# w_out as seven block products per pair of chunks in a decoder layer on one Trainium2 core

## The chip, the core and the metric

The kernel runs on one core of a Trainium2 chip. The metric is the device time of one execution in microseconds, taken as the median of several runs. Names of engines: PE is TensorE, DVE is VectorE, ACT is ScalarE, POOL is GpSimd and SP is SyncE, which only issues transfers here.

## The reference

The reference is one decoder layer on 256 tokens of width 2048 in float32: a half-step SwiGLU feed-forward stage, a mixer of two attention branches, a second feed-forward stage, each followed by a layer norm. Cut to the part that changes:

```python
h = _layer_norm(ALPHA * h + 0.5 * _swiglu(h, ffn1_w_gate, ffn1_w_up, ffn1_w_down), ln1_g, ln1_b)
...
y = sigmoid(gate_mla) * (o_mla @ w_br_mla) + sigmoid(gate_diff) * (o_diff @ w_br_diff)
mix = y @ w_out                       # (256, 2048) @ (2048, 2048)
h = _layer_norm(ALPHA * h + mix, ln2_g, ln2_b)
h = _layer_norm(ALPHA * h + 0.5 * _swiglu(h, ffn2_w_gate, ffn2_w_up, ffn2_w_down), ln3_g, ln3_b)
```

## The kernel before

**Products.** The 256 tokens are two halves, b = 0 and 1. A matrix product runs over chunks of 512 output columns and over units of two k tiles (256 rows of the weight matrix). Every float32 operand is split into a high part, rounded by ACT (L149), and a low rest, subtracted by DVE (L150). `triple` (L202 to L204) then issues three matmuls of 128x128 by 128x512 for each pair of tiles, so a unit has 12 matmuls for both halves.

**Units.** `project` makes a chunk out of units. Each unit has a load of 512 KB on SP's queue (L227), a preparation (the split into a pair of tiles taken from a ring) and its products. The ring holds 6 pairs in the mixer and w_out, and more (`widen`) where the products for b = 1 run behind those for b = 0 by `lag` units, so that the layer norm of b = 0 lies beside the products of b = 1. `look` says how many units are loaded and prepared ahead. `later(n, f)` puts a step n units further down the program. The framework may still order ready instructions of an engine among each other.

**Seven block products.** In the gate and up projections of the feed-forward stages two chunks are made together. `Seven` and `Hybrid` treat k tiles 0 to 7 as a 2x2 block product (two token halves, two groups of four k tiles, two chunks) done in seven products instead of eight, and k tiles 8 to 15 as plain units. `Seven` makes the sums of activation blocks in five steps (tiles `fa`, `fb`, `xs`). `Hybrid.group` loads the weight blocks 11, 12, 21 and 22 into `sraw` (two tiles each), adds blocks on DVE (L316: 12 and 22 and 21 onto others, eight additions of 128x1024 a group), splits them, and copies four partial results out of the PSUM banks X and Z with ACT (`snap`, L293 and L294), which `done` later adds or subtracts. The two halves s = 0, 1 of a block product have 6 matmuls each.

**Turning.** The results of some projections stand with tokens in rows and are needed with tokens in columns. `turn` does this by DMA: DVE transposes blocks of 32x32 (L405), four transfers of POOL's queue write them to DRAM (L407), one reads them back (L419), and a number of units later ACT or DVE uses them (L427 or L149). `rows_to_quad` does it on PE instead, four transposes to a quad of four k tiles (L370).

**Mixer and w_out.** The mixer projects q, k, v and the gates and does the attention heads between the units. `branch(f)`, for f = 0 to 3, multiplies the branch results by the gates on DVE (L892, L895, L896) and gives 512 columns of y, which is quad f of the input of w_out: quads 0 to 2 are turned by DMA, quad 3 by PE. Then all pending steps are flushed, and w_out is four chunks of eight plain units. `LayerNorm` loads the residual z (L445, scaled by ACT at L446) and the gain and bias `gb` (L450); `evac` adds a bank to z and takes its statistics (L464, L468); after the last chunk of a half `apply` norms it and transposes it for the second feed-forward stage.

Of the kernel before, what the change touches and what calls it, by code (L numbers as in the profile page):

```python
# [11 lines left out]
F32 = mybir.dt.float32  # L12
# [6 lines left out]
P = 128  # L19
# [11 lines left out]
G = 2  # L31
# [28 lines left out]
def layer_kernel(ctx: ExitStack, tc: tile.TileContext, a: dict, out: bass.AP):  # L60
# [212 lines left out]
    class Hybrid:  # L273


        def __init__(self, x, seven, k_tiles):
            self.x, self.seven, self.k_tiles = x, seven, k_tiles
            self.raws = {n: [act_tile([P, 1024], F32, "sraw") for _ in range(2)] for n in ("11", "12", "21", "22")}
            self.snaps = [[act_tile([P, 2, 512], F32, "snap") for _ in range(2)] for _ in range(2)]
            self.turn = 0  # L280

        def group(self, w0, w1, done):
            banks = {}
            snap = [t[:, i, :] for t in self.snaps[self.turn % 2] for i in range(2)]
            self.turn += 1
            n1, n2, n3, q5 = snap
# [9 lines left out]
                     4: lambda: done(0, 1, banks["W"], n3, ALU.subtract)}  # L296
            stops = {1, 5, 6, 7, 2, 4}
# [7 lines left out]
            def seventh(p, s):  # L305
                load_block, src, add, b = plan[p]
                st = {}

                def load():
                    w, j0 = blocks[load_block]  # L310
                    nc.sync.dma_start(R[load_block][s], w[j0 + s])

                def prep():
                    t = R[src][s]
                    if add is not None:
                        V.tensor_tensor(out=t, in0=t, in1=R[add[1]][s], op=ALU.add)  # L316
                    pair = next_pair()
                    split(*pair, t)
                    st["pair"] = [v.rearrange("p (g n) -> p g n", g=G) for v in pair]

                def now():
                    o, first = bank(b)
                    wh, wl = st["pair"]
                    xh, xl = self.seven.at_[p]
                    for g in range(G):
                        k = 2 * s + g
                        triple(o, xh[:, k, :], xl[:, k, :], wh[:, g, :], wl[:, g, :], first and g == 0,
                               s == 1 and g == 1 and p in stops, b in "XZ")
                    if s == 1 and p in after:
                        after[p]()  # L330
                unit(load if load_block else None, prep, now)

            def plain(n, j, last=False):
# [12 lines left out]

                def now():
                    wh, wl = st["pair"]
                    for b in range(2):
                        o, first = bank(names[b])  # L350
                        for g in range(G):
                            k = 2 * j + g
                            triple(o, self.x.at(0, k, b), self.x.at(1, k, b), wh[:, g, :], wl[:, g, :],
                                   first and g == 0, last and g == 1, n == 1)
                    if last:
                        done(1, 0, banks["Z"], n2, ALU.add)
                        done(1, 1, banks["X"], q5, ALU.add)
                unit(load, prep, now)
# [54 lines left out]
    def turn(row, use, wait):  # L413
# [9 lines left out]
    def turn_to_quad(row, b, x, q, wait):  # L423
        turn(row, lambda t: x.put(q, b, t), wait)

    def turn_to_cols(row, dst, b, wait):
        turn(row, lambda t: S.copy(dst[:, :, b * P:(b + 1) * P].rearrange("p k (i c) -> p k i c", i=4), t), wait)  # L427

    class LayerNorm:
# [28 lines left out]
        def evac(self, c, b, bank):  # L458
# [10 lines left out]
            if c == 3:  # L469
                self.apply(b)  # L470

# [232 lines left out]
    def mixer(x):  # L704
# [8 lines left out]
        def c_norm(b, i):  # L713
# [9 lines left out]
            later(2, lambda: turn_to_quad(c, b, cn, i, 6))  # L723
# [23 lines left out]
        def cols_proj(w, xx, kt, name, k0=0):  # L747
# [22 lines left out]
        def qr_done(b, bank):  # L770
# [3 lines left out]
            later(1, lambda: turn_to_cols(t, qrT, b, 5))  # L774
        project(a["wuq"][2], cn, 4, 512, qr_done)
        kT = [cols_proj(a["wuk"][c], cn, 4, "kT", 4) for c in range(2)]
# [111 lines left out]
        def branch(f):  # L888
# [5 lines left out]
            def done1(b, bank):  # L894
                V.tensor_tensor(out=g1[:, b, :], in0=bank, in1=g1[:, b, :], op=ALU.mult)  # L895
                V.tensor_tensor(out=g0[:, b, :], in0=g0[:, b, :], in1=g1[:, b, :], op=ALU.add)  # L896
                if f < 3:
                    later(1, lambda: turn_to_quad(g0[:, b, :], b, yq, f, 4))
# [10 lines left out]
        for f in range(4):  # L909
            branch(f)  # L910
# [70 lines left out]
def _layout(i):  # L981
# [29 lines left out]
    r["w_out"] = _chunks(np.concatenate([_turned_rows(w["w_out"][:1536]), w["w_out"][1536:]]), 512)  # L1011
# [34 lines left out]
```

## Time and profile before

| What | Value |
|---|---|
| Median of three runs | 2028.31 us (2028.13, 2028.31, 2032.78) |
| Profiled execution | 2032.79 us, its span 2031.0 us |
| Instructions | 25081, of them 8976 matmuls |
| Busy share of the span | PE 99%, DVE 75%, ACT 57%, POOL 11% |
| Mean granted TensorE clock | 0.995 |
| DMA | 446.84 MB, mean 220 GB/s |

A row of groups gives line, engine, operation, tiles and count, then the busy time, the mean of one in ns and the idle time before it. A row of a window gives start and end, the length, the busy times with counts of PE, PEld (weight loads), DVE, ACT and POOL, the granted clock, the busy share of the DMA engines and GB/s. A row of waits gives who waited for whom, the sum in us, the count and the longest. A row of DMA issues ends with the KB of one and the median time from issue to landing in us. A busy PE is not a PE at its peak: the modelled duration of a matmul overlaps the next one.

### The profile page before, as it was taken

Reading aid. Unit: us, or ns where it says so; the run is one execution under the profiler, and the core shown is the slowest. Engines: PE = TensorE matmul, PEld = TensorE weight load, DVE = VectorE, ACT = ScalarE, POOL = GpSimd, SP = SyncE. Lnnn points to the kernel's source line nnn. Section 1 sums busy time; section 2 is a strip of 40 time slices with the busy share of each in tenths; the row PEclk is TensorE's granted clock in tenths of the full one; section 3 lists DMA queues with packets and bytes.
Section 4 is the critical chain, followed back from the end, with each engine's and each line's share of the span. In section 5 each row is a group of like instructions: output and inputs, shape, how many; then the busy total and the mean of one; then the engine's idle time right before and its main releaser. Section 6 shows DMA issues by size and latency. Waiting matters only on the chain.

```text
span 2031.0 us, 25081 instructions
## 1 busy us (share of the span) xinstructions
PE 2005.3 (99%) x8976; PEld 1660.6 (82%) x8976; DVE 1529.2 (75%) x1793; ACT 1151.6 (57%) x1443; POOL 224.1 (11%) x419
## 2 busy tenths in 40 slices
PE   8999999999999999999999999999999999999997
PEld 7788888887888888888888887878888888888886
DVE  6999999997554686665665555699999999964555
ACT  5666666666333565555674445476666666653332
POOL 0111001112000012620001100001100110220000
PEclk9999999999999999999999999999999999999999
DMA  8766766668655757964456667666776667686664
GB/s 285 233 221 222 243 227 200 214 219 300 206 193 192 245 186 242 301 227 156 156 175 213 214 202 267 214 234 220 244 241 226 198 213 239 206 308 190 196 196 136
DMA packets 129501, 446.84 MB, mean 220 GB/s; under 512 B 18704, under 2 KB 18784, under 8 KB 129376
## 3 DMA queue, kind: packets, MB, share of 16 engines
q1 hardware_dynamic: 108000, 387.50, 57.0%
q0 software_dynamic: 20224, 55.65, 8.7%
q10 hardware_dynamic: 1152, 2.10, 0.3%
q8 instruction: 70, 1.15, 0.2%
q14 instruction: 55, 0.45, 0.1%
HBM read 420.00 MB, written 25.17 MB: 219 GB/s over the span
## 4 chain that ended last, share of the span: by engine, by line
PE 93%; DMA 3%; DVE 1%; ACT 1%; issue 1%; POOL 0%; DVEq 0%; ACTq 0%; SPq 0%; POOLq 0%
PE mm L202 30%; PE mm L203 30%; PE mm L204 30%; DMA xraw<-in_xT_dram 1%; DMA gb<-in_ln_g_dram 1%; DMA turned<-turn 1%; DVE wring L150 1%; ACT wring L149 0%; PE tr L370 0%; DMA sraw<-in_gu_dram 0%; DMA z<-res 0%; PE tr L791 0%; PE tr L820 0%; PE tr L789 0%; DVE sraw L316 0%
## 5 line engine op out<-in xcount | busy, mean ns | idle before, releaser
L150 DVE TENSOR_TENSOR wring<-raw,wring 128x1024 fp32r<-128x1024 f32 (+1 forms) x582 | 701.8, 1209 | 410.3 <-ACT wring L149 405.6
L149 ACT CAST wring<-raw 128x1024 fp32r<-128x1024 f32 (+1 forms) x582 | 604.5, 1043 | 541.8 <-PE mm L204 465.7
L202 PE MATMUL mm<-wring,h 128*128 128x512 f32 (+2 forms) x1632 | 634.3, 389 | 0.3 <-ACT wring L149 0.3
L204 PE MATMUL mm<-wring,h 128*128 128x512 f32 (+2 forms) x1632 | 630.1, 386 | 0.0
L203 PE MATMUL mm<-wring,h 128*128 128x512 f32 (+2 forms) x1632 | 629.3, 386 | 0.8 <-DVE wring L150 0.8
L203 PEld LDWEIGHTS mm<-wring,h 128*128 128x128 f32 x1632 | 306.7, 188 | 62.3 <-DVE wring L150 2.0
L204 PEld LDWEIGHTS mm<-wring,h 128*128 128x128 f32 x1632 | 306.6, 188 | 62.2 <-DVE h L150 1.0
L202 PEld LDWEIGHTS mm<-wring,h 128*128 128x128 f32 x1632 | 306.7, 188 | 61.6 <-ACT h L149 1.0
L149 ACT CAST wring<-sraw 128x1024 fp32r<-128x1024 f32 x280 | 290.2, 1052 | 110.7 <-PE mm L204 68.9
L150 DVE TENSOR_TENSOR wring<-sraw,wring 128x1024 fp32r<-128x1024 f32 x280 | 335.1, 1219 | 8.3 <-ACT wring L149 6.0
L202 PE MATMUL mm<-wring,xs 128*128 128x512 f32 x560 | 218.7, 391 | 2.0 <-ACT snap L293 2.0
L203 PE MATMUL mm<-wring,xs 128*128 128x512 f32 x560 | 218.5, 390 | 0.0
L204 PE MATMUL mm<-wring,xs 128*128 128x512 f32 x560 | 218.3, 390 | 0.0
L316 DVE TENSOR_TENSOR sraw<-sraw,sraw 128x1024 f32<-128x1024 f32 x160 | 191.8, 1214 | 0.1
L407 POOL DMA_DIRECT2D hT<-blocks x176 | 95.5, 551 | 744.4 <-DVE blocks L405 740.1
L202 PE MATMUL mm<-wring,x 128*128 128x512 f32 x384 | 150.1, 392 | 4.8 <-ACT x L149 4.8
L203 PE MATMUL mm<-wring,x 128*128 128x512 f32 x384 | 150.1, 392 | 0.6 <-DVE wring L150 0.6
L204 PE MATMUL mm<-wring,x 128*128 128x512 f32 x384 | 149.9, 391 | 0.0
L202 PEld LDWEIGHTS mm<-wring,xs 128*128 128x128 f32 x560 | 105.5, 188 | 24.2 <-ACT snap L293 2.4
L204 PEld LDWEIGHTS mm<-wring,xs 128*128 128x128 f32 x560 | 105.5, 188 | 22.0
L203 PEld LDWEIGHTS mm<-wring,xs 128*128 128x128 f32 x560 | 105.6, 188 | 21.9
L407 POOL DMA_DIRECT2D turn<-blocks x112 | 61.0, 552 | 378.2 <-DVE blocks L405 347.8
(238 smaller groups left out, 1621.5 us busy)
## 6 DMA issues: line engine op xcount, KB each, us to landing
raw<-in_gu_dram SPq DMA_DIRECT2D x192, 512.0 KB, 4.3
raw<-in_dn_dram SPq DMA_DIRECT2D x176, 512.0 KB, 4.2
sraw<-in_gu_dram SPq DMA_DIRECT2D x160, 512.0 KB, 5.2
raw<-in_wgm_dram SPq DMA_DIRECT2D x32, 512.0 KB, 3.3
raw<-in_wgd_dram SPq DMA_DIRECT2D x32, 512.0 KB, 3.6
raw<-in_w_out_dram SPq DMA_DIRECT2D x32, 512.0 KB, 3.5
hT<-blocks POOLq DMA_DIRECT2D x176, 64.0 KB, 2.5
hraw<-hT POOLq DMA_DIRECT2D x44, 256.0 KB, 3.9
```

The source lines that it names most:

```text
L149: S.copy(hi, src)
L150: V.tensor_tensor(out=lo, in0=src, in1=hi.bitcast(F32), op=ALU.subtract)
L202: PE.matmul(o, xh, wh, start=first, stop=False, skip_group_check=again)
L203: PE.matmul(o, xh, wl, start=False, stop=False, skip_group_check=again)
L204: PE.matmul(o, xl, wh, start=False, stop=last, skip_group_check=again)
L316: V.tensor_tensor(out=t, in0=t, in1=R[add[1]][s], op=ALU.add)
L407: nc.gpsimd.dma_start(to.rearrange("(g r) (i f) -> i r g f", g=4, i=4)[i], t[32 * i:32 * (i + 1), :].rearrange("r (g f) -> r g f", g=4))
```

## The change

- w_out becomes two groups of two chunks by `Hybrid.group`, with seven block products for k tiles 0 to 7 and plain units for k tiles 8 to 15. Quads 0 and 1 of y are turned by DMA and kept as raw tiles for `Seven`; quad 2 is now turned by PE like quad 3. The host lays out w_out's rows accordingly.
- There are no snaps in w_out. `LayerNorm.fold` adds or subtracts a partial result from bank X or Z to z on DVE, right after products 1, 6, 7 and 5.
- Half of the block sums are made by adding transfers: after the preparation of product 5 a transfer of POOL's queue adds block 22 from DRAM onto the tile of block 12 (for product 7), after that of product 6 block 21 onto the tile of block 11 (for product 4).
- The layer norm and `Seven` are set up before the last branch, with a ring of 5; nothing is flushed between the branch and w_out. In the last group the plain units of the second chunk come last, the products for b = 1 four units behind those for b = 0.
- In `turn` the transfer back is issued `wait` units on, and the use follows `more` units after it: 4 and 10 (8 for k, 8 for the normed q and kv rows) instead of 4 and 5 (5 and 6); the heads start two units later.

```diff
     class Hybrid:
-        def __init__(self, x, seven, k_tiles):
+        def __init__(self, x, seven, k_tiles, snaps=True, adds=None):
+            self.adds = adds or {}
...
-        def group(self, w0, w1, done):
+        def group(self, w0, w1, done, fold=None, last_group=False):
...
+            if fold is not None:
+                after = {1: lambda: fold(0, 0, banks["X"], -1.0), 6: lambda: fold(1, 0, banks["X"], 1.0),
+                         7: lambda: fold(0, 1, banks["X"], -1.0), 5: lambda: fold(1, 1, banks["Z"], 1.0),
+                         2: lambda: done(0, 0, banks["Y"]), 4: lambda: done(0, 1, banks["W"])}
...
-                    if add is not None:
+                    if add is not None and (src, add[1]) not in self.adds.values():
                         V.tensor_tensor(out=t, in0=t, in1=R[add[1]][s], op=ALU.add)
                     pair = next_pair()
                     split(*pair, t)
...
+                    if p in self.adds:
+                        to, block = self.adds[p]
+                        w, j0 = blocks[block]
+                        nc.gpsimd.dma_start(R[to][s], w[j0 + s], accum_op=ALU.add)
...
+                if last_group and n == 1:
+                    unit(load, prep, lambda: half(0), lambda: half(1))
+                else:
+                    unit(load, prep, now)
...
+            if last_group:
+                for p, js in ((1, (4,)), (5, (5,)), (6, (6,)), (7, (7,)), (2, ()), (4, ()), (3, ())):
+                    for s in range(2):
+                        seventh(p, s)
+                    for j in js:
+                        plain(0, j)
+                look(0, 0)
+                lag[0] = 4
+                for j in range(4, end + 1):
+                    plain(1, j, j == end)
+                return
...
-    def turn(row, use, wait):
+    def turn(row, use, wait, more):
...
-            later(wait, lambda: use(turned(t)))
-        later(wait - 1, back)
+            later(more, lambda: use(turned(t)))
+        later(wait, back)
...
+        def fold(self, c, b, bank, sign):
+            z = self.z[b][c // 2][:, (c % 2) * 512:(c % 2) * 512 + 512]
+            V.scalar_tensor_tensor(out=z, in0=bank, scalar=sign * self.scale, in1=z, op0=ALU.mult, op1=ALU.add)
...
-            later(2, lambda: turn_to_quad(c, b, cn, i, 6))
+            later(2, lambda: turn_to_quad(c, b, cn, i, 4, 8))
...
-                later(1, lambda: turn_to_cols(t, dst, b, 5))
+                later(1, lambda: turn_to_cols(t, dst, b, 4, more))
...
-                later(10 + 3 * h + 2 * i, f)
+                later(12 + 3 * h + 2 * i, f)
...
-                if f < 3:
-                    later(1, lambda: turn_to_quad(g0[:, b, :], b, yq, f, 4))
+                if f < 2:
+                    later(1, lambda: turn(g0[:, b, :], lambda t: S.copy(
+                        yq.raw(f, b).rearrange("p (k i c) -> p k i c", k=4, i=4), t), 4, 6))
...
         for f in range(4):
+            if f == 3:
+                before_last(yq)
             branch(f)
...
-    yq = mixer(h1)
-    catch_up(0)
-    flush()
     h2 = Acts(KD, "h2", (0, 1))
-    ln = LayerNorm(1.0, res[0], a["ln2_g"], a["ln2_b"], keep(1), h2, (a["ln2_gc"], a["ln2_bc"]))
-    for c in range(4):
-        project(a["w_out"][c], yq, KD, 512, lambda b, bank, c=c: ln.evac(c, b, bank),
-                hook=at_unit(0, widen) if c == 3 else None)
+    out_stage = {}
+
+    def before_out(y):
+        narrow_to(5)
+        out_stage["ln"] = LayerNorm(1.0, res[0], a["ln2_g"], a["ln2_b"], keep(1), h2, (a["ln2_gc"], a["ln2_bc"]), (0, 16))
+        seven = out_stage["seven"] = Seven(y)
+        for i, f in enumerate(seven.steps):
+            later(2 + i, f)
+
+    yq = mixer(h1, before_out)
+    ln = out_stage["ln"]
+    narrow_to(6)
+    look(3, 4)
+    hy = Hybrid(yq, out_stage["seven"], KD, False, {5: ("12", "22"), 6: ("11", "21")})
+    for p in range(2):
+        hy.group(a["w_out"][2 * p], a["w_out"][2 * p + 1], lambda n, b, bank, p=p: ln.evac(2 * p + n, b, bank),
+                 lambda n, b, bank, sign, p=p: ln.fold(2 * p + n, b, bank, sign), p == 1)
+    widen()
```

More of the change, by code (lines that the diff above doesn't have):

```diff
@@ L345, in prep, with half @@
                     st["pair"] = [v.rearrange("p (g n) -> p g n", g=G) for v in pair]
-                def now():
[L348 to L358, printed above, removed]
-            end = self.k_tiles // G - 1
+                def half(b):
+                    wh, wl = st["pair"]
+                    o, first = bank(names[b])
+                    for g in range(G):
+                        k = 2 * j + g
+                        triple(o, self.x.at(0, k, b), self.x.at(1, k, b), wh[:, g, :], wl[:, g, :],
+                               first and g == 0, last and g == 1, n == 1)
+                    if last and fold is not None:
+                        done(1, b, o)
+                    elif last:
+                        done(1, b, o, (n2, q5)[b], ALU.add)
+                def now():
+                    half(0)
+                    half(1)
+                if last_group and n == 1:
+                    unit(load, prep, lambda: half(0), lambda: half(1))
+                else:
+                    unit(load, prep, now)
+            end = self.k_tiles // G - 1
+            if last_group:
[9 more added lines that the diff above has]
+                return
             for p, n, j in ((1, 0, 4), (5, 0, 5), (6, 0, 6), (7, 0, 7), (2, 1, 4), (4, 1, 5), (3, 1, 6)):
@@ L702, in p_cols, with mixer @@
         return pt
-    def mixer(x):
+    def mixer(x, before_last):
         c_row = [act_tile([P, 1024], F32, "c_row") for _ in range(2)]
```

24 lines of the change are left out of this document (13 added, 11 removed).

## The prediction

> **What bounds the kernel now.** I read the page first: its table of busy times and the chain that ended last. Then PE's waits, then the windows and timelines of PE and DVE around the stage that changes, then the table of DMA issues.
>
> ```profile
> PE 2005.3 (99%) x8976; PEld 1660.6 (82%) x8976; DVE 1529.2 (75%) x1793; ACT 1151.6 (57%) x1443; POOL 224.1 (11%) x419
> ...
> PE mm L202 30%; PE mm L203 30%; PE mm L204 30%; DMA xraw<-in_xT_dram 1%; DMA gb<-in_ln_g_dram 1%; DMA turned<-turn 1%; DVE wring L150 1%; ACT wring L149 0%; PE tr L370 0%; DMA sraw<-in_gu_dram 0%; DMA z<-res 0%; PE tr L791 0%; PE tr L820 0%
> ```
> Nine tenths of the chain are the three matmul lines L202 to L204. So a microsecond is worth something only where PE issues fewer matmuls or stands still less. PE's idle time against others is short:
>
> ```profile
> PE tr L370 <- DVE gate L896: 2.8, 1, 2.8
> PE mm L202 <- ACT snap L293: 2.0, 1, 2.0
> ...
> PE tr L675 <- DVE kr_row L670: 1.3, 1, 1.3
> ...
> PE mm L202 <- ACT v L761: 0.9, 1, 0.9
> ```
> The first of these is the start of w_out. The columns of a timeline are start, duration, engine, line, operation, tiles and count.
>
> ```profile
> 1227.73 0.39 PE L202 MATMUL mm<-wring,od 128*128 128x512 f32 x1
> ...
> 1230.90 0.39 PE L204 MATMUL mm<-wring,od 128*128 128x512 f32 x1
> 1234.06 0.69 PE L370 MATMUL tr<-ident,gate 128*128 128x128 f32 x4 [2.77 <-DVE gate L896]
> 1234.44 0.74 PE L202 MATMUL mm<-wring,y 128*128 128x512 f32 x1
> ...
> 1237.94 0.39 PE L204 MATMUL mm<-wring,y 128*128 128x512 f32 x1
> ...
> 1238.87 0.60 PE L370 MATMUL tr<-ident,gate 128*128 128x128 f32 x4
> 1239.23 0.48 PE L202 MATMUL mm<-wring,y 128*128 128x512 f32 x1
> ```
> From 1227.73 to 1230.90 are 14 steps: one matmul costs 3.17/14 = 0.2264 us (the 0.39 us of a row overlaps the next). After the wait, eight matmuls come at about 0.43 us. From 1230.90 to 1237.94 are 7.04 us for nine steps (2.04 us) and four transposes (0.36 us, by 1238.87 to 1239.23): 4.64 us are lost. The wait's cause is DVE:
>
> ```profile
> 1231.36 1.23 DVE L150 TENSOR_TENSOR wring<-raw,wring 128x1024 fp32r<-128x1024 f32 x1 [0.81 <-ACT wring L149]
> 1232.50 0.68 DVE L895 TENSOR_TENSOR gate<-mm,gate 128x512 f32<-128x512 f32 x1
> 1233.22 0.69 DVE L896 TENSOR_TENSOR gate<-gate,gate 128x512 f32<-128x512 f32 x1
> ```
> The last gate products can be read shortly after 1230.90, DVE is busy with a split, then makes two gate operations, and only then can PE transpose. PE has nothing else, since w_out's first product is emitted behind the flush.
>
> **The change part by part.**
>
> *Fewer matmuls.* w_out is one group of three lines:
>
> ```profile
> L202 PE MATMUL mm<-wring,y 128*128 128x512 f32 x128 | 50.8, 397 | 0.0
> ```
> That is 3 x 128 = 384. A new group has seven block products of 2 x 6 and eight plain units of 12: 84 + 96 = 180, two groups 360. 24 matmuls go: 24 x 0.2264 = -5.43 us, on PE, nothing hides it.
>
> *Start of w_out.* The first two units are now block products on rows of quads 0 and 1, whose Seven steps are done during branch 3; quads 2 and 3 are needed only from the third and the ninth unit. The 4.64 us go if those units' splits are ready. I take -4.64; what is late next is the load and split of block 11, priced in a rival.
>
> *Transposes.* Quad 2 goes from DMA to PE: two sets of four at 0.36 us: +0.72 us. Its eight stores and two loads leave POOL's queue.
>
> *Seven's five steps in branch 3.* Four differences of at most 0.69 us, three splits of 1.13, one negation of 0.69: about 6.8 us of DVE, and on ACT four copies. The cover is DVE's idle time in that branch:
>
> ```profile
> 1198.00:1231.00 33.00, 33.00 (x147) 27.23 (x146) 20.29 (x22) 13.63 (x15) 9.65 (x18) 1.00 0.77 243
> ```
> The third busy time is DVE's, 20.29 of 33 us: 12.7 are idle, so I cost it at nothing; if that cover were gone, it would cost the 6.8. The z loads and their scaling on ACT move ahead too, the first half scaled four and six units into a branch of eight, and the first fold comes two units after it; the four gb loads move into the first group, where nothing waits for them until the norm.
>
> *DVE in the groups.* A group needs 22 splits (14 for block products, 8 for plain units) and four additions of 128x1024, four folds, four evacuations and four statistics of 128x512.
>
> ```profile
> 198.76 4.62 DVE L150 TENSOR_TENSOR wring<-sraw,wring 128x1024 fp32r<-128x1024 f32 x4
> ...
> 210.25 0.69 DVE L526 TENSOR_TENSOR gus<-mm,snap 128x512 f32<-128x512 f32 x1
> ```
> and the window of such a group in the feed-forward stage:
>
> ```profile
> 190.30:231.10 40.80, 40.80 (x182) 33.78 (x181) 40.22 (x42) 26.17 (x30) 4.09 (x8) 1.00 0.65 216
> ```
> Four splits in 4.62 us, the last of 1.22: (4.62 - 1.22)/3 = 1.133 us each. 26 x 1.133 + 12 x 0.69 = 37.8 us, against 180 x 0.2264 = 40.75 on PE. In the window, with eight additions on DVE, DVE is busy 40.22 of 40.8 and PE is never late; counted in the same overlapping way the new group has 26 x 1.22 + 8.3 = 40.0. So DVE fits, with 3.0 us to spare; with all eight additions (another 4.5) it would not. The new evacuations by DVE (four folds, where ACT copied) have a cover of one plain unit, 12 x 0.2264 = 2.7 us, before PE writes bank X again after products 6 and 7. Behind a run of splits like the 4.62 a fold could come 4.62 + 0.69 - 2.7 = 2.6 late, four times in all: 0 to 10.4 us. DVE already reads banks in the feed-forward groups, and no such wait stands among PE's, so I take +1.0, near the low end.
>
> *The adding transfers.* After product 5's preparation a transfer adds block 22 onto 12, after product 6's one adds 21 onto 11, two halves each; eight transfers of 512 KB. They wait in POOL's queue for DVE's addition; behind them stand only norm loads. ACT's copy for product 7, or 4, waits for the landing. Between lie, on DVE, nine operations of 1.133 (six splits and three additions, for products 5 and 6 and two plain units): 10.2 us. The trace has no adding transfer; plain ones of that size are
>
> ```profile
> raw<-in_w_out_dram SPq DMA_DIRECT2D x32, 512.0 KB, 3.5
> ...
> z<-res POOLq DMA_DIRECT2D x8, 512.0 KB, 8.2
> gb<-in_ln_g_dram POOLq DMA_DIRECT2D x6, 512.0 KB, 13.8
> ...
> gain<-in_c_gain_dram POOLq DMA_DIRECT2D x1, 512.0 KB, 5.1
> ```
> 3.5 us from SP, and on POOL's queue 5.1 alone, 8.2 with four at once, 13.8 for rows spread over all partitions. What is late is paid at four places, less 2 x 3.0 us that DVE has to spare and about 6.8 us of ring (five block units of 6 x 0.2264): loss = 4 x (L - 10.2) - 12.8, if positive. At 5.1, 8.2 and 13.8 it is 0, 0 and 1.6. I take L near 10, above the 8.2 because a sum is read as well as written, and no loss; the ends go on in the rivals. The Trainium skill (Collectives: The Full Stack, section "The bandwidth ceiling: the fold count and why AG ≠ RS ≠ AR") says that a reduction in the DMA reads two sources and measured about half a copy's rate; no run here shows it.
>
> *Longer trips.* Rows of PE's timeline show what they can give:
>
> ```profile
> 840.86 0.39 PE L204 MATMUL mm<-wring,cn 128*128 128x512 f32 x1
> 842.16 0.50 PE L202 MATMUL mm<-wring,cn 128*128 128x512 f32 x1 [0.91 <-ACT v L761]
> ```
> 1.30 us instead of 0.2264: ACT's queue had stood before a turned row and then copied v late. With the use five units later this goes: -1.07 us. If the late kr_row (1.3 above) went too, another 1.1; against it, the six small tiles are held longer, and each of the ten trips of q and k could cost such a wait (+10.7). I take -1.07, as that wait is the one shown.
>
> *The tail.* The chain from the last product for b = 0 to the first product of the next stage:
>
> ```profile
> 1316.57 0.68 DVE L464 TENSOR_TENSOR z<-mm,z 128x512 f32<-128x512 f32 x1
> ...
> 1318.19 1.17 DVE L150 TENSOR_TENSOR wring<-raw,wring 128x1024 fp32r<-128x1024 f32 x1
> ...
> 1319.51 1.23 DVE L150 TENSOR_TENSOR wring<-raw,wring 128x1024 fp32r<-128x1024 f32 x1
> ```
> and on PE:
>
> ```profile
> 1325.45 0.50 PE L202 MATMUL mm<-wring,h 128*128 128x512 f32 x1
> ```
> 8.9 us, in which PE had six half units for b = 1 (36 matmuls, 8.2 us) and transposes. The new order leaves four half units: 12 matmuls, 2.7 us, less cover. Two splits (1.17 and 1.23) stand inside the chain and may fall away: 0 to 2.7 us, I take +1.5. A wait of about 2 us has a further price:
>
> ```profile
> 74.99 0.39 PE L204 MATMUL mm<-wring,x 128*128 128x512 f32 x1
> 77.33 0.79 PE L202 MATMUL mm<-wring,xs 128*128 128x512 f32 x1 [1.95 <-ACT snap L293]
> ...
> 80.85 0.40 PE L204 MATMUL mm<-wring,xs 128*128 128x512 f32 x1
> ```
> 5.86 us for nine steps: 3.82 lost, of which the eight slow ones are 3.52 - 1.81 = 1.71. So the upper end is 2.7 + 1.7 = 4.4. The Trainium skill (TensorE: Matmul & The Clock Gate, section "What's actually happening") puts the fall of the clock at an idle window of about 3.4 us; by it the end would stay 2.7. The row, a wait of 1.95 us, goes against that, and I keep 4.4.
>
> *Sum.* -5.43 - 4.64 + 0.72 + 1.0 - 1.07 + 1.5 = -7.9 us. The profiled execution took 2032.79 us (span 2031.0 and 1.8 around it), 4.5 above the median 2028.31 of the runs shown, which go from 2028.13 to 2032.78; the edit touches nothing that I can tie this spread to. So 2024.9 for the profiled one, 2020.4 for the median.
>
> **The rivals.**
> *Adding transfers decide, slower.* Each of the four landings holds ACT's queue, DVE behind it, then PE in the middle of each group. Slower by 0.3% (6.1 us, about what a measurement of this kernel can tell from no change) needs a loss of 7.9 + 6.1 = 14.0: L over 16.9 us. At L = 20 it is 26.4 us: 2046.8. For it: POOL's 13.8 and DMA engines already 0.65 busy in such a group. Against: 5.1 alone.
> *Adding transfers cost twice a plain one.* L = 2 x 8.2 = 16.4: 12.0 us lost, 2032.4, within 0.3%. The skill's Collectives page, as cited, stands beside this one; the traces neither bear it out nor exclude it.
> *New stalls at both ends.* w_out's first group starts as the first one of the kernel did at 77.33 (3.82), and the tail costs 4.4 instead of 1.5: 2020.4 + 3.8 + 2.9 = 2027.1, within 0.3%. For it: DVE is nearly full in the groups and must prepare block products early. Against: the start lies behind a branch where DVE idles a third of the time.
> *The trips change nothing*, if ACT's queue keeps its order: 2021.5, inside my forecast's range.
>
> **How the numbers follow.** Forecast 0.58: 2020.4, own range 2016.8 (no tail, no fold, both mixer waits gone: -11.5) to 2025. Faster by over 0.3% means under 2022.2; of the 0.58, 0.45 lies there and 0.13 within. Twice a plain one 0.10, within. Both ends 0.12: 0.11 within, 0.01 slower. Late landings 0.20, slower. Faster 0.45, same 0.34, slower 0.21. Range 2015.5 to 2038: it takes in the second and third case and landings up to 17.8 us, and leaves about half of the slower case out, with a little below.
>
> **What would show it.** Right: 360 matmuls on y and xs in the stage; no gate wait in PE's list and no 0.43 us matmuls at its start; adding transfers landing under 10 us and no ACT wait for sraw before products 7 and 4 above 3 us; a PE gap of 0 to 3 us before the first product on h. Wrong: landings over 14 us, PE waiting for folds in bank X more than once a group, PE late on a split of sraw, or waits on small tiles in the q and k projections.

## The result and the profile after

The kernel after takes 2044.07 us (median of six runs, 2038.89 to 2048.8), the kernel before beside it 2030.92 us (six runs, 2028.13 to 2034.21). The ratio is 1.0065, with a 95% interval of 1.0051 to 1.0079. So the change made the kernel slower by some 13 us where 8 us less were forecast, and the time lies above the range given. The profiled execution of after took 2045.07 us, 12.3 more than that of before.

The table of busy times, two rows of groups and the table of DMA issues of after show that the change did what it says:

```profile
PE 2006.5 (98%) x8960; PEld 1660.3 (81%) x8960; DVE 1556.7 (76%) x1823; ACT 1166.8 (57%) x1459; POOL 225.7 (11%) x417
...
L202 PE MATMUL mm<-wring,xs 128*128 128x512 f32 x616 | 240.9, 391 | 5.8 <-ACT wring L149 4.1 <-ACT snap L296 1.7
L202 PE MATMUL mm<-wring,y 128*128 128x512 f32 x64 | 25.4, 400 | 0.7 <-ACT wring L149 0.7
...
sraw<-in_w_out_dram POOLq DMA_DIRECT2D x8, 512.0 KB, 6.0
gb<-in_ln_g_dram POOLq DMA_DIRECT2D x6, 512.0 KB, 13.2
```

8960 matmuls are 8976 less 24, with 8 transposes more. The plain units on y have 3 x 64, the block products on xs 3 x 56 more than before's 560: 360 in all. The eight adding transfers land in 6.0 us at the median. What went wrong stands in PE's list of waits (the columns are the sum in us, the count and the longest):

```profile
PE mm L202 <- ACT wring L149: 10.8, 3, 6.0
PE mm L202 <- ACT x L149: 4.6, 1, 4.6
...
PE tr L732 <- DVE p L828: 2.5, 1, 2.5
PE tr L708 <- DVE kr_row L703: 2.0, 1, 2.0
```

The wait for the gate is gone. In its place come 10.8 us for pairs of the ring that ACT copied late, in three places, and 2.5 us for the first attention head's p. (The 4.6 us for x are the start of the kernel, 4.8 before.)

**The start of w_out.** PE's, ACT's, POOL's and DVE's timelines of after around the largest but one of these waits:

```profile
1248.55 0.39 PE L204 MATMUL mm<-wring,y 128*128 128x512 f32 x1
1253.07 0.79 PE L202 MATMUL mm<-wring,xs 128*128 128x512 f32 x1 [4.13 <-ACT wring L149]
...
1259.10 0.40 PE L204 MATMUL mm<-wring,xs 128*128 128x512 f32 x1
```

```profile
1244.04 0.58 ACT L149 CAST y<-tr 128x512 fp32r<-128x512 f32 x1
1249.13 1.06 ACT L481 ACTIVATE gb<-gb 128x1024 f32<-128x1024 f32 x1 [4.51 <-DMA gb<-in_ln_g_dram]
1250.10 3.87 ACT L149 CAST wring<-sraw 128x1024 fp32r<-128x1024 f32 x4
```

```profile
1238.60 0.89 POOL L330 DMA_DIRECT2D sraw<-in_w_out_dram  x1 [35.62 <-PE mm L204]
1239.73 0.87 POOL L330 DMA_DIRECT2D sraw<-in_w_out_dram  x1 [0.24 <-issue]
1240.28 1.42 POOL L479 DMA_DIRECT2D gb<-in_ln_g_dram  x2
```

```profile
1236.83 2.35 DVE L323 TENSOR_TENSOR sraw<-sraw,sraw 128x1024 f32<-128x1024 f32 x2
```

From 1248.55 to 1259.10 are 15 steps, 3.40 us at 0.2264 each; they took 10.55, so 7.15 us are lost, 4.13 of waiting and the rest in matmuls at 0.43 us. ACT stood for 4.51 us before the halving of gb, with four copies of sraw behind it in its queue. And the gb loads were late: in POOL's queue they stand behind the first two adding transfers, and these wait for DVE's two additions for product 5, the last operations that read the tile of block 12. The additions end at about 1238.05 and 1239.18 us, each some 0.55 us before a transfer is issued.

**The tail.** The timelines of PE, ACT and SP at the end of w_out in after:

```profile
1329.20 0.65 PE L399 MATMUL tr<-ident,z 128*128 128x128 f32 x4
1335.87 0.80 PE L202 MATMUL mm<-wring,h 128*128 128x512 f32 x1 [6.02 <-ACT wring L149]
...
1341.06 0.40 PE L202 MATMUL mm<-wring,h 128*128 128x512 f32 x1
```

```profile
1324.37 0.20 ACT L413 ACTIVATE sd<-ve 128x1 f32<-128x1 f32 x1 [7.74 <-DVE ve L411]
...
1334.69 1.13 ACT L149 CAST wring<-raw 128x1024 fp32r<-128x1024 f32 x1
```

```profile
1312.53 27.12 SPq L227 DMA_DIRECT2D raw<-in_gu_dram  x6
```

Four transposes take 0.36 us, so the first product on h was due at 1329.56, and the tenth 2.04 us later, at 1331.60. It came at 1341.06: 9.5 us late. The weights of the next stage had been asked for since 1312.53, and ACT idled for 7.74 us, but it copied the first of them at 1334.69, behind the norm. The ring is widened only behind the whole last group, so those preparations stand behind the norm in the program; e2 below tests this.

### The profile page after: what moved, and what is told of

The parts are those of the page before. It is cut to its first block, busy times and chain, and to the rows that moved or that the text cites. A ratio compares the mean times of both kernels' runs of the same rounds, so it can differ in the third digit from the quotient of the medians.

```text
span 2043.3 us, 25092 instructions
## 1 busy us (share of the span) xinstructions
PE 2006.5 (98%) x8960; PEld 1660.3 (81%) x8960; DVE 1556.7 (76%) x1823; ACT 1166.8 (57%) x1459; POOL 225.7 (11%) x417
## 5 line engine op out<-in xcount | busy, mean ns | idle before, releaser
L150 DVE TENSOR_TENSOR wring<-raw,wring 128x1024 fp32r<-128x1024 f32 (+2 forms) x566 | 682.0, 1209 | 388.8 <-ACT wring L149 384.1
L149 ACT CAST wring<-raw 128x1024 fp32r<-128x1024 f32 (+2 forms) x566 | 588.7, 1043 | 523.3 <-PE mm L204 439.9
L149 ACT CAST wring<-sraw 128x1024 fp32r<-128x1024 f32 x308 | 319.0, 1052 | 135.3 <-PE mm L204 79.9
L150 DVE TENSOR_TENSOR wring<-sraw,wring 128x1024 fp32r<-128x1024 f32 x308 | 368.7, 1219 | 15.6 <-ACT wring L149 13.0
L202 PE MATMUL mm<-wring,xs 128*128 128x512 f32 x616 | 240.9, 391 | 5.8 <-ACT wring L149 4.1
L203 PE MATMUL mm<-wring,xs 128*128 128x512 f32 x616 | 240.4, 390 | 1.1 <-DVE wring L150 1.1
L204 PE MATMUL mm<-wring,xs 128*128 128x512 f32 x616 | 240.2, 390 | 0.0
L323 DVE TENSOR_TENSOR sraw<-sraw,sraw 128x1024 f32<-128x1024 f32 x168 | 201.3, 1214 | 0.1
L202 PEld LDWEIGHTS mm<-wring,xs 128*128 128x128 f32 x616 | 116.0, 188 | 30.8 <-ACT wring L149 4.6
L203 PEld LDWEIGHTS mm<-wring,xs 128*128 128x128 f32 x616 | 116.1, 188 | 25.6 <-DVE wring L150 1.5
L204 PEld LDWEIGHTS mm<-wring,xs 128*128 128x128 f32 x616 | 116.0, 188 | 24.2
L436 POOL DMA_DIRECT2D turn<-blocks x104 | 56.6, 552 | 315.5 <-DVE blocks L434 274.9
```

The source lines that it names most:

```text
L149: S.copy(hi, src)
L150: V.tensor_tensor(out=lo, in0=src, in1=hi.bitcast(F32), op=ALU.subtract)
L202: PE.matmul(o, xh, wh, start=first, stop=False, skip_group_check=again)
L203: PE.matmul(o, xh, wl, start=False, stop=False, skip_group_check=again)
L204: PE.matmul(o, xl, wh, start=False, stop=last, skip_group_check=again)
L436: nc.gpsimd.dma_start(to.rearrange("(g r) (i f) -> i r g f", g=4, i=4)[i], t[32 * i:32 * (i + 1), :].rearrange("r (g f) -> r g f", g=4))
```

## The experiments

Each ratio is against the kernel before, measured beside it (medians 2029.6 to 2031.0 us); a thousandth is 2.03 us.

**e1, the old trips.** The kernel after with the turned rows due, and the heads started, as before:

```diff
-            later(2, lambda: turn_to_quad(c, b, cn, i, 4, 8))
+            later(2, lambda: turn_to_quad(c, b, cn, i, 5, 6))
...
-                later(1, lambda: turn_to_cols(t, dst, b, 4, more))
+                later(1, lambda: turn_to_cols(t, dst, b, 4, 5))
...
-            later(1, lambda: turn_to_cols(t, qrT, b, 4, 10))
+            later(1, lambda: turn_to_cols(t, qrT, b, 4, 5))
...
-                later(12 + 3 * h + 2 * i, f)
+                later(10 + 3 * h + 2 * i, f)
...
-                        yq.raw(f, b).rearrange("p (k i c) -> p k i c", k=4, i=4), t), 4, 6))
+                        yq.raw(f, b).rearrange("p (k i c) -> p k i c", k=4, i=4), t), 3, 4))
```

> The changed kernel with the waits of the turned rows and the start of the heads as before. Theory A (three places of loss: the mixer, the start of w_out, the tail): the mixer's new waits (2.5 us on the first head with slow matmuls behind it, 2.0 on kr_row) come from the longer trips, so this gains 4 to 6 us on the changed kernel's 2044: 2039. Rival B (the trips do nothing, the mixer's waits are scatter between executions): 2044, within 1.5.

2040.81 us, 1.0042 (1.0030 to 1.0055). The wait for p is gone from PE's list; both waits of w_out stay, at 6.5 and 6.0 us. The longer trips and later heads cost after about 0.0023, which is 4.7 us by the ratios and 3.3 us by the medians, with an uncertainty of nearly 4 us.

**e2, the ring widened earlier.** One line in the last group:

```diff
                 look(0, 0)
+                widen()
                 lag[0] = 4
```

> The changed kernel with the ring widened before the last four plain units instead of after them. Theory A: the 6.0 us wait of PE on ACT's copy for the next stage goes, because ACT can copy next-stage weights while it waits for the norm; with its slow matmuls that is 6 to 8 us: 2037. Rival B (the tail is the norm's own chain with too little cover, as the prediction had it): at most 1 to 2 us are gained: 2042 to 2043.

2037.83 us, 1.0026 (1.0016 to 1.0036). Its list of PE's waits:

```profile
PE mm L202 <- ACT wring L149: 6.3, 2, 5.6
...
PE tr L400 <- DVE z L526: 1.4, 1, 1.4
...
PE mm L204 <- DVE h L150: 0.9, 1, 0.9
...
PE tr L400 <- ACT h2raw L405: 0.5, 1, 0.5
...
PE mm L202 <- ACT h L149: 0.2, 1, 0.2
```

The wait of 6.0 us at the tail is gone; what is left for wring is the start. In its place PE waits four times for the norm and its first results (z, h2raw and the two parts of h), 3.0 us in all. So most of the tail's loss was the ring, not the norm's length: 6.2 us by the medians, 7.9 by the ratios.

**e3, the gain halved on DVE.** The halving leaves ACT's queue and is put into a step of the norm that runs anyway:

```diff
+            self.halve = at == (0, 16)
...
-                if i == 0:
+                if i == 0 and at != (0, 16):
                     later(4, lambda: S.mul(t, t, 0.5))
...
-                V.tensor_tensor(out=zs[c], in0=zs[c], in1=gs[c], op=ALU.mult)
+                if self.halve:
+                    V.scalar_tensor_tensor(out=zs[c], in0=zs[c], scalar=0.5, in1=gs[c],
+                                           op0=ALU.mult, op1=ALU.mult)
+                else:
+                    V.tensor_tensor(out=zs[c], in0=zs[c], in1=gs[c], op=ALU.mult)
```

> The changed kernel with the halving of the second norm's gain moved from ACT, where it waits for a load of 13 us, into the norm's last step on DVE. Theory A: ACT's 4.5 us wait for that load goes and with it PE's 4.3 us stall in w_out's first group and the slow matmuls behind it, 5 to 7 us: 2038. Rival B (DVE is too full at the start for six splits and four additions in time): the stall stays, 2044. Rival C (adding transfers): the stall moves to products 7 and 4, 2044.

2037.1 us, 1.0030 (1.0021 to 1.0039). PE's timeline at the start of w_out:

```profile
1243.16 0.39 PE L204 MATMUL mm<-wring,y 128*128 128x512 f32 x1
1245.71 0.50 PE L202 MATMUL mm<-wring,xs 128*128 128x512 f32 x1 [2.15 <-ACT wring L149]
1246.04 0.40 PE L202 MATMUL mm<-wring,y 128*128 128x512 f32 x1
```

Half of the wait and all of the slow matmuls behind it are gone. In the traces the loss at this place falls from 7.15 to 2.4 us; by the medians the kernel is 7.0 us faster, and the intervals of the two ratios take in both figures. A wait of 2.15 us stays.

**f1, the trips alone.** The kernel before with the longer trips and the later heads, without seven products.

> The kernel before with only the longer trips and the later heads. Theory A: slower by 4 to 6 us in the mixer: 2035. The prediction's step (trips gain 1.07): 2029. Rival B (scatter): 2030 to 2031, no difference.

2029.09 us, 0.9993 (0.9984 to 1.0002): no change that can be told. Its list of waits holds what the trips give and take:

```profile
PE tr L699 <- DVE p L795: 2.1, 1, 2.1
PE tr L675 <- DVE kr_row L670: 1.6, 1, 1.6
```

The wait for the gate at the start of w_out is not in it, but the one for p is. Two effects work against each other in this trace: from the last product on od to the first one on h it takes 4.5 us less than in before, and from the last product on cn to the first one on om, where the heads are, 2.5 us more (209.30 in place of 206.82). Theory A, 4 to 6 us slower, fell; the time is the 2029 of the prediction's step, but by other terms than that step had.

**f2, the trip of the branch's y alone.** The kernel before with this one trip made longer: the transfer back four units on, the use six units behind it.

```diff
-                    later(1, lambda: turn_to_quad(g0[:, b, :], b, yq, f, 4))
+                    later(1, lambda: turn_to_quad(g0[:, b, :], b, yq, f, 4, 6))
```

> The kernel before, with the longer trip for the branch's turned y alone, and nothing else of the change. Theory A (the wait for the gate ahead of w_out, 2.8 us and eight slow matmuls, 4.6 us in all, goes because the y rows are turned earlier in the order; the first head's wait comes from the other trips): 2026 to 2027, 0.998, no wait for the gate and none for VectorE's p over 1 us. Theory B (the y trip moves nothing by itself): 2030, the wait for the gate stays at 2.8 us.

2027.68 us, 0.9984 (0.9975 to 0.9994): 0.16% faster than before, and faster than after. ACT's timeline of before, and PE's of this kernel:

```profile
1226.59 0.62 ACT L149 CAST y<-turned 128x512 fp32r<-128x512 f32 x1 [3.61 <-DMA turned<-turn]
```

```profile
1232.32 0.60 PE L370 MATMUL tr<-ident,gate 128*128 128x128 f32 x4
```

In before ACT stood 3.61 us before a turned row, its copies for the ring behind it, and DVE's splits and gate operations behind those. In f2 it no longer does at that place, and PE transposes without a wait. From the last product on od to the first one on h it takes 90.10 us (1232.09 to 1322.19) in place of 94.55 (1230.90 to 1325.45), 4.45 less, which is about what the prediction read off that wait (4.64). So the wait that was credited to the block products goes without them.

**g1, both cures.** The edits of e2 and e3 together.

> The kernel after with both cures at once: the ring of arrivals widened before the last group's pieces, and the norm's gain halved on VectorE inside the last step of the norm instead of on ScalarE. Theory A (two separate waits, one at the start of w_out and one at its end, each worth 6 to 7 us): the gains add, 2044.1 - 6.2 - 7.0 = about 2031, the waits of matmuls for ScalarE's wring below 3 us in all and no slow matmuls at either place. Theory B (the two cures buy the same time, the weights' queue running ahead): about 2037, as with one of them.

2032.56 us, 1.0011 (1.0001 to 1.0021). Theory A holds in the main: the time lies near its 2031 us and not at 2037, the waits for wring are 3.0 us in all, and no slow matmuls follow at either place. The two together give 0.0054, the two alone 0.0039 and 0.0035; the 0.0020 between them is no larger than what the four intervals leave open.

**g2, both cures and the old trips.** The edits of e1, e2 and e3.

> The kernel before this one in the list, with the old trips for turned rows as well (turned rows due as in the kernel before the change, heads at 10). Theory A (three separate losses: start of w_out, its end, first head): 2031 - 3.3 = about 2027 to 2028, below the kernel before (2030.4) by what 24 fewer matmuls are worth less what is left at the start of w_out (2 to 3 us); the waits for VectorE's p and kr_row below 1 us. Theory B (the longer trips are worth something once the other waits are gone): not below the kernel with both cures and the longer trips.

2029.18 us, 0.9996 (0.9987 to 1.0005). All that after had lost is back, 0.0069 or 14 us, but not the 8 us that the prediction had on top. At the start of w_out PE still waits 3.25 us. The timelines of ACT, DVE and POOL there, and the first two adding transfers with who waited for them:

```profile
1239.23 1.05 ACT L149 CAST wring<-sraw 128x1024 fp32r<-128x1024 f32 x1 [2.47 <-DMA sraw<-in_w_out_dram]
1242.30 2.94 ACT L149 CAST wring<-sraw 128x1024 fp32r<-128x1024 f32 x3 [2.02 <-DMA sraw<-in_w_out_dram]
```

```profile
1244.33 2.36 DVE L150 TENSOR_TENSOR wring<-sraw,wring 128x1024 fp32r<-128x1024 f32 x2 [3.14 <-ACT wring L149]
```

```profile
1245.85 0.87 POOL L330 DMA_DIRECT2D sraw<-in_w_out_dram  x1 [9.92 <-DVE wring L150]
```

```profile
L330 POOL DMA_DIRECT2D sraw<-in_w_out_dram x2: 872/879/886, 1230.7 to 1231.9; - x2
...
  ACT wring L149: 4.5, 2
...
DMA to landing us min/median/max: 8.4/9.2/10.0
```

These two landed in 8.4 and 10.0 us, and ACT waited for both. The median of all eight in this trace, 7.0 us, does not show them. The rows also show the order in ACT's queue. The two copies that wait are those for product 7, which the first two transfers serve. DVE's splits at 1244.33 are those for product 6, since the next adding transfer, which needs product 6's first split, goes out as that split ends. They were released by the third of the four copies. So ACT copies for product 7 ahead of product 6, which PE needs first, and PE's 3.25 us end with that third copy.

**g3, no adding transfers.** The kernel g1 with all eight block sums on DVE (`adds=None`).

> The kernel with both cures, but all eight block sums added by VectorE and none by an adding transfer. It leaves nothing of the computation out. Theory A (the adding transfers are cheap and relieve VectorE in a stretch in which it is short): 3 to 8 us slower than the kernel with both cures, with more waits of matmuls for VectorE's wring in w_out. Theory B (my rival, adding transfers late): faster than it by 2 us or more.

2037.45 us, 1.0035 (1.0023 to 1.0048): 5 us slower than g1, as theory A has it. No wait over 0.8 us is left at the start of w_out, but at its end PE waits 6.6 us for the norm's z: DVE, busy in 97.4 of the 100 us from 1230 to 1330, is too full.

**h1 and g4, gb earlier; g5, gb later.** Kernel h1 is the kernel after with the gb loads from the second step of branch 3 on, g4 is g2 with the same, and g5 is g2 with 26 in place of 2.

```diff
-        out_stage["ln"] = LayerNorm(1.0, res[0], a["ln2_g"], a["ln2_b"], keep(1), h2, (a["ln2_gc"], a["ln2_bc"]), (0, 16))
+        out_stage["ln"] = LayerNorm(1.0, res[0], a["ln2_g"], a["ln2_b"], keep(1), h2, (a["ln2_gc"], a["ln2_bc"]), (0, 2))
```

> The kernel after with one number changed: the norm's four gain and shift rows (gb) are loaded from the second step of branch 3 on, not from the sixteenth, which was the start of w_out; the halving stays on ScalarE. Theory A (at the start of w_out the DMA engines are full, share 1.02 to 1.03 there against 0.53 to 0.74 in the branch, and the gb loads of 512 KB are part of it; the halving stood in ScalarE's queue for them): the wait of 4.5 us and the slow matmuls behind it go, 2044 - 6 to 8 = 2036 to 2038, the DMA share of the start falls below 1. Theory B (the ring of five and VectorE's additions alone make it late): as with the gain on VectorE, 2 to 3 us of wait stay, 2037 at best.

> The kernel with both cures and the old trips, and gb loaded from the second step of branch 3 on. Theory A (the wait of 3.3 us and eight slow matmuls that are left at the start of w_out come from loads of sraw that land late, ScalarE waits 2.5 and 2.0 us for them, because gb and the adding transfers fill the DMA engines): 2029.2 - 3 to 5 = 2024 to 2026. Theory B (the adding transfers and the first loads of w_out fill the engines without gb): 2029.

> The same kernel, but gb loaded from the twenty-sixth step on, ten steps behind the start of w_out. Theory A: the wait at the start goes as well, 2025 to 2027, if nothing else is then met: the share of the DMA engines is 1.04 and 0.81 there. Theory B: 2029, or slower, as loads of the second group's blocks come late instead.

2042.69 us, 1.0071 (1.0055 to 1.0087), 2036.52 us, 1.0037 (1.0022 to 1.0051), and 2030.44 us, 1.0002 (0.9991 to 1.0013). Theory A fell for early loads: PE's wait at the start grew to 8.0 us in h1 and 7.2 in g4, g4 is 0.0041 slower than g2, and h1 cannot be told from after. The line of the adding transfers in g4:

```profile
L330 POOL DMA_DIRECT2D sraw<-in_w_out_dram x4: 851/880/1137, 1231.4 to 1251.2; - x4
...
  ACT wring L149: 8.4, 2
DMA to landing us min/median/max: 5.4/9.6/14.3
```

One of them took 14.3 us, and ACT waited 8.4 us for two. The last gb load, though due in the branch, was released only at 1230.91, right ahead of them. Why they land so much later than in g2 is not settled.

For late loads g5 settles nothing, because its edit did not move them. POOL's timeline of g5:

```profile
1233.51 0.89 POOL L330 DMA_DIRECT2D sraw<-in_w_out_dram  x1 [35.63 <-PE mm L204]
...
1235.19 1.42 POOL L481 DMA_DIRECT2D gb<-in_ln_g_dram  x2
```

The first two gb loads go out 2.2 us behind the last product on od (1232.97), right behind the adding transfers. In g2 it is 2.3 us (1232.48 against 1230.20), at the same place in the queue. In this respect g5 is g2 run again: the wait at the start, 3.25 us in g2 and 1.47 in g5, scatters between executions by that much, and the times do not differ.

**k1, i1 and j1, the first group's sums on DVE.** Adding transfers only in the last group: k1 is after with that edit, i1 is g2 with it, j1 is i1 with the longer y trip.

```diff
+            adds = self.adds if last_group else {}
...
-                    if p in self.adds:
+                    if p in adds:
```

> The kernel after with this one edit: in the first group all block sums by VectorE. Theory A (two things hold the start of w_out, the halving of gb in ScalarE's queue and the adding transfers, and either of them is enough to make it late): 2041 to 2044, with the wait at the start shorter but still there. Theory B (the adding transfers alone): the wait goes, 2036 to 2038. Theory C (the halving alone, which taking it away left at 2.5 us): no change, 2044.

> The kernel with both cures and the old trips, but in the first group of w_out all block sums are added by VectorE; the second group keeps its adding transfers. Theory A (at the start of w_out the adding transfers land late, 8.4 and 10.0 us in that kernel and 11.1 and 14.3 us with gb in the branch, against 5.2 to 7.0 later, and ScalarE, VectorE and TensorE wait for them; with all sums on VectorE that start had a wait of 0.6 us): the wait of 3.3 us, the eight slow matmuls and the 0.8 us behind them go, 2029.2 - 5 = 2024 to 2025, below both kernels. Theory B (VectorE, with 2.4 us more additions in that group, is late into the second one): 2028 to 2031.

> The same, and the longer trip for the branch's turned y, the one part that was worth something alone (0.9984). Theory A (that trip only removed the wait for the gate, which block products at the start of w_out do not have anyway): no change against the kernel ahead of it in the list, within 1 us. Theory B (it also frees ScalarE's queue in the branches): 1 to 3 us faster than it.

k1: 2037.32 us, 1.0040 (1.0027 to 1.0054). The wait at the start is gone, with the halving still on ACT: theory B. POOL's timeline shows how:

```profile
1230.20 0.53 POOL L480 DMA_DIRECT2D gb<-in_ln_g_dram  x1 [31.69 <-PE mm L204]
```

With no adding transfer ahead of it in the queue the first gb load goes out 3.4 us ahead of the last product on od (1233.60), in after 2.2 us behind it (1240.28 against 1238.06): 5.6 us earlier in the stage. The four land in 5.0 to 7.9 us, in after in 8.8 to 12.0. ACT halves them without waiting. How much of this is the place in the queue and how much the freer DMA engines k1 does not separate.

i1: 2031.04 us, 1.0008 (1.0000 to 1.0017), and j1: 2031.32 us, 1.0008 (0.9999 to 1.0017). The start is cured here too, and still the time is not below g2's: theory B. (Four more additions at 1.133 us are 4.5 us more for DVE, not the 2.4 of the expectation.) PE's timeline of i1 at the tail, and DVE's busy time (the third) in the same 100 us of before, after, g2 and i1. They begin within 1 us of the last product on od, in after 8 us ahead of it:

```profile
1318.93 3.80 PE L401 MATMUL tr<-ident,z 128*128 128x128 f32 x16 [5.40 <-DVE z L528]
```

```profile
1230.00:1330.00 100.00, 97.11 (x430) 79.23 (x429) 65.10 (x76) 52.90 (x66) 0.55 (x1) 0.98 0.68 234
```

```profile
1230.00:1330.00 100.00, 95.01 (x416) 77.38 (x414) 82.73 (x94) 52.99 (x58) 9.08 (x12) 0.97 0.75 230
```

```profile
1230.00:1330.00 100.00, 92.30 (x403) 73.88 (x402) 90.39 (x106) 62.24 (x77) 10.04 (x14) 0.98 0.82 248
```

```profile
1230.00:1330.00 100.00, 93.34 (x408) 75.86 (x407) 97.49 (x119) 62.06 (x77) 5.80 (x9) 0.97 0.73 231
```

DVE was busy 65.1 of 100 us before and 97.5 in i1. What the start gains, the norm's z gives back at the end, with a wait of 5.40 us in place of 1.7 in g2. The longer y trip adds nothing where there is no wait for the gate.

## Why the prediction was wrong, point by point

**Right.** 24 matmuls fewer; no gate wait; DVE fits in the groups with four of the eight sums and does not with all eight (g3); adding transfers land in 6.0 us at the median in after, where 10 were assumed. The folds, +1.0 forecast, cost little: no wait of PE for them stands in after's list, and one of 0.4 to 0.6 us in g1 to g5.

**The start of w_out: -4.64 forecast, which fell on two steps.** First, the gb loads were costed at nothing, since "nothing waits for them until the norm". ACT's halving of them does, 4.51 us, with the copies of the next block products behind it. The prediction named the loads that stand behind the adding transfers in POOL's queue, and did not ask who waits for those loads. k1 shows that without the adding transfers the halving delays nothing. So 4.64 were gained and 7.15 lost at one place. The rival of a new stall at the start had put 3.8 on it. Second, the 10.2 us of DVE's work between an adding transfer and its use were wrong for the first group. In g2 the first adding transfer is issued at 1230.7, ACT has nothing else to do from about 1236.8 (1239.23 less its 2.47 us of waiting), and so some 6 us lie between. The formula let product 7's copy follow the work for products 5 and 6 and two plain units; in ACT's queue it stands ahead of product 6's copies, which then wait with it. Landings of 8.4 and 10.0 us are late there, though the formula gave no loss below 13.4. The rival of late adding transfers thus has its mechanism right at the start of the first group, at shorter landings than it needed. In after, taking them out of the first group gains 0.0025, some 5 us (k1). Once the halving is off ACT's queue it gains nothing more: without them in the first group (i1) or at all (g3) the time is no better than in g2 or g1, as DVE then is late elsewhere.

**The tail: +1.5 forecast, at most 4.4, and 9.5 measured.** The forecast counted the matmuls that cover the norm, and took it that the next stage's first pair is ready when h is. ACT had the time for it but not the order. The step that failed is that the forecast put the preparation of the next stage's weights, which needs a wider ring, at nothing. With the ring widened earlier (e2) the waits for the norm come to 3.0 us, twice the term and within its upper end.

**The trips: -1.07 forecast.** v's wait of 0.9 went, but one of 0.5 for kTr came at the same place, and the products on cn take 41.43 us in place of 41.78: 0.35 gained. Against it the first head's p comes late, 2.5 us in after. With the longer trips and later heads that wait is 0.7 to 2.5 us in seven traces and absent in one (h1); in the eight traces without them it is never there. From the last product on cn to the first one on om it takes 206.8 to 206.9 us in those eight, and 206.9 (h1) to 211.0 us (after) in the others, 1.8 us more on average. e1 and g2 price the trips and heads at 3 to 5 us by the times, with wide intervals. The prediction had allowed for waits on the small tiles in general, not for the heads, which it let start two units later at no cost. Which of the two, the later rows or the later heads, makes p late was not taken apart. The wait for kr_row (1.3 before, 2.0 in after) proves nothing: with the old trips it goes from 0.3 us (e1) to 3.1 (j1).

**What the sum comes to.** The same stretches of the two profiled executions, from one matmul to the same one of the other, differ by -1.1 us up to the products ahead of kr_row, +2.1 around kr_row, -0.35 on cn, +4.2 in the heads, +7.7 from the first product on om to the first block product of the second feed-forward stage, and -0.25 behind it. That is 12.3, the difference measured. In the +7.7 stand -5.43 for matmuls, -4.64 for the gate, +0.72 for transposes, +7.15 for the start and +9.5 for the tail, 7.3 together, and 0.4 more that is not listed. The first two stretches are scatter as far as can be told, since they move by as much between executions with the same code there.

**Is there a gain in it at all?** With all three causes removed, g2 is at 0.9996 (0.9987 to 1.0005), and the piece of the change that needs no block products, f2, is at 0.9984. In this study no form of the seven products beat f2. They shorten PE by 5.4 us and fill DVE from 65 to 90 or 97 us in 100, with a norm at the end that needs DVE. Even in g1's trace, which has the shortest such stage with seven products, the six waits of over 0.4 us between the last product on od and the first block product of the second feed-forward stage come to 5.5 us and so eat what the matmuls save. From the first product on om to that block product it takes 311.6 us in g1, 309.5 in f2 and 314.0 in before.

**The clock.** The prediction weighed a rule of the Trainium skill (TensorE: Matmul & The Clock Gate, section "What's actually happening", an idle window of about 3.4 us) against a row with a wait of 1.95 us and eight slow matmuls behind it. The runs are between the two. In after, slow matmuls follow waits of 2.0 us (kr_row) and 2.5 us (p); in e3 a wait of 2.15 us has none behind it, nor has one of 2.4 us (kr_row) in h1. The granted clock is 0.50 in after from 1253.6 to 1258.6 us, in the slow matmuls, and 1.00 in e3 from 1245.7 to 1248.7, behind its wait. That page also says that the window runs freely, so that the point of the change shifts. That fits one and the same length of wait having both outcomes; that waits far below 3.4 us are enough is what the traces show and the rule does not.

## What to carry to other kernels

Where an operation is put ahead of others in a queue, follow what it delays to the end: here DVE's additions held the adding transfers, these the gb loads, these one halving on ACT, and this TensorE. A buffer pool that is enlarged between two stages also decides when the next stage may be prepared; enlarge it before the work that is to hide the seam. And before matmuls are traded for vector work, count what VectorE has in that very stage, with the norm behind it: 24 matmuls saved were not worth 25 to 32 points of its time.

## What was not expected of the hardware

An adding transfer lands as fast as a plain one when it has room, but holds the DMA engines more than twice as long. In after the adding transfers land in 6.0 us at the median, and SP's plain loads of w_out into the same tiles in 6.0:

```profile
sraw<-in_w_out_dram SPq DMA_DIRECT2D x16, 512.0 KB, 6.0
```

From 1280 to 1304 us POOL's queue (q0) carries four adding transfers and nothing else, and SP's (q1) plain loads alone. The rows give packets, MB and the share of the engines' time:

```profile
q0 software_dynamic: 576, 2.10, 54.7%
q1 hardware_dynamic: 715, 2.61, 28.4%
```

A MB costs 6.3 us of all 16 engines' time by adding transfers and 2.6 us by plain loads, 2.4 times as much; in g2 from 1262 to 1300 us it is 2.3 times. The Trainium skill (Collectives: The Full Stack, section "The bandwidth ceiling: the fold count and why AG ≠ RS ≠ AR") puts a reduction that reads two sources at half the rate of a copy. The engines' time here agrees roughly with that, the landing of a single transfer does not show it. Where the DMA engines were full at the start of w_out (share 1.02 from 1225 to 1235 us in g2, from 1235 to 1245 in h1 and g4) the first two adding transfers took 8.4 and 10.0 us in g2 and up to 14.8 in h1, though 6.4 and 8.0 in after at share 1.03. The plain loads of the same tiles were late to a lesser degree, up to 9.3 us in g2 and 11.4 in h1. That the engines' time of the adding transfers makes them late there is likely, but no run shows it.
